# S5 tables' products and weighted adaLN sums on VectorE alone, with a four-operation S5 scan step on GpSimd, in a two-layer hybrid diffusion backbone

## The chip, the cores and the metric

One core of one Trainium2 chip runs the whole program. The metric is device microseconds for one execution. PE is TensorE (with PEld for its weight loads), DVE is VectorE, ACT is ScalarE, POOL is GpSimd, SP is the engine whose queue issues most of the DMAs.

## The reference

Two layers work on 512 tokens of 1024 channels: 256 of context and 256 of latents. Each layer takes a shift, a scale and a gate from the conditioning vector (one for the latents, another for the context), modulates an RMSNorm with them, projects it to all inputs of three mixers, merges the mixers by gates, and runs a SwiGLU FFN with the same kind of modulation:

```python
for l in range(DEPTH):                                   # DEPTH = 2
    mod = (silu_c @ w_ada[l] + b_ada[l])[:, None, :]     # 1024 -> 6 x 1024, latents
    mod_c = silu_cc @ w_ada[l] + b_ada[l]                # the same for the context
    ...
    u, rk, rv, nk, nv, rq, rg, nq, gates = split_cols(h @ w_in[l], IN_SPLIT)
    ...
    y_s5, y_s5_c = s5_mixer(u, cu, ...)    # both directions, 32 groups, 64 complex states each
    ...                                    # retention, neighbourhood attention, merge, FFN
```

The S5 mixer is a linear recurrence x[t] = a x[t-1] + B u[t] with complex a, forward and backward in time, followed by a read-out with C. All is fp32.

## The kernel before

**Weights.** Every weight is read once from HBM, in chunks of 512 KB (128 partitions x 1024 values) that SP's queue fetches into four raw buffers (L373). `w` turns a chunk into two fp32r tensors: the high part is a cast on ScalarE (L383), the low part a subtraction on VectorE (L384). `mm3` then issues three matmuls for each block of 128x128 weights: high by high (L389), high by low (L390), low by high (L391). So each chunk that is multiplied costs one ScalarE and one VectorE instruction over 128x1024 values, and TensorE waits for both.

**S5.** The recurrence is cut into chunks of eight tokens. Tables of products of powers of a with B (`s5_e`) and with C (`s5_g`, called by `s5_kwins` and `s5_out`) let TensorE do the work inside a chunk; `_prods` builds them, for four blocks of groups in each layer and each table. One call of `_prods` covers two directions, d = 0 and 1, with three instructions each: two products (L742, L743) and their sum or difference (L744), over 128x1024 values for `s5_e` and 128x1152 for `s5_g`. Direction 0 runs on VectorE and direction 1 on GpSimd. TensorE transposes the `s5_e` tables (L759); it multiplies the `s5_g` tables in `s5_kwin` (L1150). What is left between chunks is a scan of 64 steps (`s5_scan`), both directions at once, wholly on GpSimd: from the second step on, each takes three instructions over 128x64 values (L1094 to L1096) and two over 128x32 (L1097, L1098). After the last step the scan swaps halves of its result through memory called "swap": two DMAs (L1103, L1104) and two copies of 64x2112 values (L1105, L1106). It runs beside the neighbourhood attention's projections in each layer.

**adaLN of the second layer.** `ada_sum` runs beside the FFN of the first layer: 40 chunks of w_ada (five rounds of eight) are weighted by a column of the conditioning vector and summed, one sum for each of two vectors (s = 0 and 1). The first chunk of a round is a ScalarE multiplication (L559). For the other 35, s = 1 is one VectorE multiply-add (L561), while s = 0 is a ScalarE multiplication into a temporary (L565) and a GpSimd addition (L566). A few matmuls (L572) reduce the sums over the partitions.

**The order of the work.** The program is written as generators. `weave` interleaves a main generator with side generators at given rates (for the FFN of the first layer: `rest`, with `s5_e` and `s5_kwins` of the second layer, at 0.5, and the adaLN at 0.9). Buffers come from an allocator written for this kernel. A scheduler then sets the order on each engine's queue from its own estimate of the times. Each engine takes its queue strictly in order. `take(ada, ...)` in the second layer draws on the generator of `ada_sum`.

```python
weave(self.ffn(l, lambda: self.norm(l + 1, 0, [0, 1])), (rest(), 0.5), (chain(ada, self.adas), 0.9))
```

Of the kernel before, what the change touches and what calls it, by code (L numbers as in the profile page):

```python
# [13 lines left out]
ALU = mybir.AluOpType  # L14
# [51 lines left out]
def _consts():  # L66
# [27 lines left out]
def _layout(inp):  # L94
# [105 lines left out]
def mk(ap, off, dims):  # L200
    return bass.AP(ap.tensor, ap.offset + off, [list(ap.ap[0])] + [list(d) for d in dims])


def weave(main, *sides):

    acc = [0.0] * len(sides)
    live = [True] * len(sides)

    def step(i):
        try:  # L210
            next(sides[i][0])
        except StopIteration:
            live[i] = False

    for _ in main:
        for i, (_, each) in enumerate(sides):
            acc[i] += each
            while live[i] and acc[i] >= 1.0:
                acc[i] -= 1.0
                step(i)  # L220
    while any(live):
        for i in range(len(sides)):
            if live[i]:
                step(i)
# [6 lines left out]
def chain(*gens):  # L231
    for g in gens:
        yield from g


class Net:
# [10 lines left out]
    def run(self, stack):  # L247
        tc, nc = self.tc, self.nc
        NR = 8192 + 6 * 1024 + 8192
        NF = 30600  # L250
        sb = stack.enter_context(tc.tile_pool(name="sb", bufs=1))
        ps = stack.enter_context(tc.tile_pool(name="ps", bufs=1, space=PSUM))
        dr = stack.enter_context(tc.tile_pool(name="dr", bufs=1, space=DRAM))
        fa = sb.tile([P, NF], F32, name="fa")
        ra = sb.tile([P, NR], F32R, name="ra")
# [26 lines left out]
        def ld(name, n):  # L282
# [31 lines left out]
                                in1=cvec.rearrange("p (k s) -> p k s", s=2), op=ALU.mult)  # L314
# [234 lines left out]
    def ada_sum(self, l, rounds):  # L549

        nc, F = self.nc, self.F
        acc = [F.alloc(1024, "acc", top=True) for _ in range(2)]
        for r in rounds:
            for k in range(8):
                t = self.wraw(("w_ada", l, r, k))
                for s in range(2):
                    c = self.c32[:, k, s:s + 1]
                    if k == 0:
                        nc.scalar.mul(acc[s].ap, t, c)  # L559
                    elif s:  # L560
                        nc.vector.scalar_tensor_tensor(out=acc[s].ap, in0=t, scalar=c, in1=acc[s].ap,  # L561
                                                       op0=ALU.mult, op1=ALU.add)
                    else:
                        p = F.alloc(1024, "adap")
                        nc.scalar.mul(p.ap, t, c)  # L565
                        nc.gpsimd.tensor_tensor(out=acc[s].ap, in0=acc[s].ap, in1=p.ap, op=ALU.add)  # L566
                        p.free()
                yield
            pt = self.misc()
            for s in range(2):  # L570
                for q in range(4):
                    nc.tensor.matmul(pt[32 * q:32 * q + 32, 0:256], self.sel[:, s * 32:(s + 1) * 32],  # L572
                                     acc[s].v(256, q * 256), start=(s == 0), stop=(s == 1))
# [155 lines left out]

    def _prods(self, dst, A, B, c0, l, blk, nb, op):  # L730

        n0 = nb - 1
        P2 = self.tabs[l][0].ap
        for d in range(2):
            tmp = self.F.alloc(nb * 128, "prod")
            eng = (self.nc.vector, self.nc.gpsimd)[d]
            po = (n0 * 64 if d else 0) + blk * 16 + d
            pd = [[2, 8], [-64 if d else 64, nb], [0, 16]]
            wo, wd = c0 + d * 16, [[32, 8], [0, nb], [1, 16]]
            o = mk(dst, d * nb * 16, [[2 * nb * 16, 8], [16, nb], [1, 16]])  # L740
            t = tmp.ap.rearrange("p (g n h) -> p g n h", g=8, n=nb)
            eng.tensor_tensor(out=o, in0=mk(P2, po, pd), in1=mk(A, wo, wd), op=ALU.mult)  # L742
            eng.tensor_tensor(out=t, in0=mk(P2, 640 + po, pd), in1=mk(B, wo, wd), op=ALU.mult)  # L743
            eng.tensor_tensor(out=o, in0=o, in1=t, op=op)  # L744
            tmp.free()
# [147 lines left out]
    def layer(self, l):  # L893
        nc, F = self.nc, self.F
# [3 lines left out]
        na = [None, None]  # L898
        self.yna = self.yslot[0]
        if l == 0:  # L900
# [16 lines left out]
            ada = self.ada(0, (2, 3, 4, 5))  # L917
# [22 lines left out]
        else:  # L940
# [10 lines left out]
            for _ in self.m_u(l):  # L951
                pass
            weave(self.m_na(l, 0, na, kpre), (chain(*(self.s5_in(l, blk) for blk in range(4)), self.s5_scan(l)), 20))
            ada = self.adas
            weave(self.m_na(l, 1, na), (self.attn(l, 0, na), 2.5), (self.take(ada, 4), 0.5))
            self.yret = self.yslot[1]
            weave(self.m_ret(l), (self.attn(l, 1, na), 1.2), (self.ret_decay(l), 0.75), (self.take(ada, 4), 0.3))
            self.swap.free()
            self.m = F.alloc(8 * n, "m", top=True)
            weave(self.branch(l, 2, self.yna, 0), (self.retention(l), 2.5), (self.take(ada, 4), 0.25))  # L960
            tg = F.alloc(8 * n, "tg", top=True)
            ys5 = self.yslot[0][:, 1024:]
            weave(chain(self.branch(l, 1, self.yret, 1), self.gates(l, 0, tg)),
                  (chain(self.s5_out(l, self.yslot[0]), self.s5_glu(l, self.yslot[0], ys5)), 1), (self.take(ada, 3), 0.15))
            self.ug.free()
            self.X.free()
            self.x_alloc()
# [5 lines left out]
        ada = self.adas  # L973
        if last:
            ada = self.ada(1, (5,))
# [6 lines left out]
        else:  # L982
            e = []
# [83 lines left out]
    def s5_scan(self, l):  # L1067


        nc = self.nc  # L1070
        e = nc.gpsimd
        xb = self.X.ap
        self.swap = self.F.alloc(2112, "swap", top=True)
        A = [mk(self.PW, (ri * 10 + 8) * 64 + l * 32, [[0, 2], [1, 2], [2, 16]]) for ri in range(2)]
        T = [self.scan_tmp.v(64, 64 * i).rearrange("p (r d g) -> p r d g", r=2, d=2) for i in range(4)]

        def at(f, r, part=None):
            dims = [[1056 + (r - f) * 16, 2], [1, 16]]
            if part is None:
                return mk(xb, f * 16, [[2112, 2]] + dims)  # L1080
            return mk(xb, part * 2112 + f * 16, dims)

        for s in range(64):
            if s < 32:
                cf, cr = s + 1, 31 - s
                pf, pr = cf - 1, cr + 1
            else:
                cf, cr = s + 2, 96 - s
                pf, pr = cf - 1, cr + 1
            if s == 32:  # L1090
                e.tensor_copy(at(33, 65), at(32, 0))
            t1, t2 = T[(s % 2) * 2], T[(s % 2) * 2 + 1]
            if s:
                e.tensor_tensor(out=t1, in0=at(pf, pr), in1=A[0], op=ALU.mult)  # L1094
                e.tensor_tensor(out=t2, in0=at(pf, pr), in1=A[1], op=ALU.mult)
                e.tensor_tensor(out=at(cf, cr), in0=at(cf, cr), in1=t1, op=ALU.add)  # L1096
                e.tensor_tensor(out=at(cf, cr, 0), in0=at(cf, cr, 0), in1=t2[:, 1], op=ALU.subtract)  # L1097
                e.tensor_tensor(out=at(cf, cr, 1), in0=at(cf, cr, 1), in1=t2[:, 0], op=ALU.add)  # L1098
            yield
        self.dump(f"S{l}", self.X.ap)  # L1100

        tm = self.swap
        e.dma_start(tm.ap[0:64], xb[64:128, 0:2112])  # L1103
        e.dma_start(tm.ap[64:128], xb[0:64, 2112:4224])  # L1104
        e.tensor_copy(xb[64:128, 0:2112], tm.ap[64:128])  # L1105
        e.tensor_copy(xb[0:64, 2112:4224], tm.ap[0:64])  # L1106
        yield
# [723 lines left out]
```

## Time and profile before

| | |
|---|---|
| median of 3 runs | 1609.64 us (1609.52 to 1610.44) |
| the profiled execution's own time | 1614.29 us |
| its span, first to last instruction | 1612.5 us |
| mean granted TensorE clock | 0.972 of full speed |
| busy: PE / DVE / ACT / POOL | 1506.2 / 1024.7 / 663.5 / 473.4 us |
| read from and written to HBM | 226 MB and 16 MB, 150 GB/s over the span |

The profile is one execution. "Busy" is the time in which an engine ran instructions; an instruction that waits for a resource inside its run counts as busy. A wait of an engine is put down to the instruction that released it. The granted clock is a share of TensorE's full speed, 2.4 GHz.

### The profile page before, as it was taken

How to read it: one execution, taken by the hardware profiler on the slowest of the kernel's cores; microseconds unless marked ns; L12 is line 12 of the kernel's file. 1: busy time of each engine (PE TensorE's matmuls, PEld its weight loads, DVE VectorE, ACT ScalarE, POOL GpSimd, SP SyncE). 2: the span in 40 equal slices, each digit the busy share in tenths (PEclk: the TensorE clock that was granted, in tenths of full speed). 3: DMA queues.
4: the chain of work that ended last, by engine and by line, in shares of the span. 5: the costliest groups of instructions: out<-in, count | busy, mean ns of one | idle time of the engine just before them, and what ended most of it. 6: DMA issues, size and time to landing. Idle time of an engine off the chain costs nothing.

```text
span 1612.5 us, 25768 instructions
## 1 busy us (share of the span) xinstructions
PE 1506.2 (93%) x10066; PEld 1272.9 (79%) x10066; DVE 1024.7 (64%) x1716; ACT 663.5 (41%) x1166; POOL 473.4 (29%) x750
## 2 busy tenths in 40 slices
PE   7968999899999999989997989999996999999997
PEld 5756677678888887777885768898785999899997
DVE  6794435657456686689588895551662765765566
ACT  4525444224422334343432343445643445454443
POOL 0083985530000020157155660005994000000000
PEclk9989999999999999999998999999997999999999
DMA  9412345564332423544444653332322686655552
GB/s 371 140 37 102 119 151 174 169 196 160 124 105 79 155 81 121 167 169 157 146 167 158 214 165 121 111 129 83 105 88 74 201 278 234 222 183 184 183 180 96
DMA packets 78587, 245.94 MB, mean 153 GB/s; under 512 B 9088, under 2 KB 22912, under 8 KB 76672
## 3 DMA queue, kind: packets, MB, share of 16 engines
q1 hardware_dynamic: 76864, 237.92, 44.0%
q0 software_dynamic: 1600, 6.36, 1.3%
q8 instruction: 79, 1.29, 0.3%
q14 instruction: 44, 0.36, 0.1%
HBM read 225.96 MB, written 16.12 MB: 150 GB/s over the span
## 4 chain that ended last, share of the span: by engine, by line
PE 67%; DVE 9%; POOL 7%; issue 7%; DMA 6%; ACT 3%; SPq 1%; DVEq 0%; POOLq 0%; ACTq 0%
PE psall L389 17%; PE psall L391 17%; PE psall L390 17%; DMA fa<-in_wst_dram 3%; DVE ra L384 3%; PE psall L867 2%; PE psall L869 2%; PE psall L868 2%; DVE fa L561 2%; POOL fa L744 1%; POOL fa L743 1%; PE psall L517 1%; PE psall L1054 1%; PE psall L1215 1%; POOL fa L1097 1%
## 5 line engine op out<-in xcount | busy, mean ns | idle before, releaser
L389 PE MATMUL psall<-ra 128*128 128x256 f32 (+1 forms) x2122 | 713.7, 341 | 18.4 <-ACT ra L383 15.4
L391 PE MATMUL psall<-ra 128*128 128x256 f32 (+1 forms) x2122 | 710.5, 338 | 13.3 <-DVE ra L384 13.3
L390 PE MATMUL psall<-ra 128*128 128x256 f32 (+1 forms) x2122 | 712.0, 337 | 0.0
L384 DVE TENSOR_TENSOR ra<-fa,ra 128x1024 fp32r<-128x1024 f32 (+1 forms) x284 | 384.1, 1355 | 296.9 <-ACT ra L383 294.8
L383 ACT CAST ra<-fa 128x1024 fp32r<-128x1024 f32 (+1 forms) x284 | 293.5, 1036 | 472.7 <-PE psall L390 249.6
L389 PEld LDWEIGHTS psall<-ra 128*128 128x128 f32 x2122 | 403.9, 192 | 74.4 <-ACT ra L383 18.2
L391 PEld LDWEIGHTS psall<-ra 128*128 128x128 f32 x2122 | 405.7, 192 | 58.4 <-DVE ra L384 17.2
L390 PEld LDWEIGHTS psall<-ra 128*128 128x128 f32 x2122 | 407.1, 192 | 41.9 <-issue 3.3
L566 POOL TENSOR_TENSOR fa<-fa 128x1024 f32<-128x1024 f32 x35 | 101.1, 2889 | 161.3 <-DMA fa<-in_wst_dram 70.7
L742 POOL TENSOR_TENSOR fa<-fa 128x1024 f32<-128x1024 f32 (+1 forms) x16 | 49.3, 3086 | 286.6 <-DVE fa L699 244.2
L561 DVE SCALAR_TENSOR_TENSOR fa<-fa 128x1024 f32<-128x1024 f32 x35 | 77.6, 2218 | 8.5 <-ACT fa L559 5.7
L867 PE MATMUL psall<-ra 128*128 128x512 f32 x192 | 76.2, 409 | 5.5 <-ACT ra L828 4.9
L868 PE MATMUL psall<-ra 128*128 128x512 f32 x192 | 75.9, 399 | 0.0
L565 ACT ACTIVATE fa<-fa 128x1024 f32<-128x1024 f32 x35 | 40.2, 1151 | 83.8 <-DMA fa<-in_wst_dram 37.1
L869 PE MATMUL psall<-ra 128*128 128x512 f32 x192 | 72.5, 400 | 0.2 <-DVE ra L829 0.2
L1698 DVE SCALAR_TENSOR_TENSOR fa<-psall,fa 128x256 f32<-128x256 f32 x96 | 43.2, 477 | 45.6 <-PE psall L391 45.4
L1094 POOL TENSOR_TENSOR fa<-fa 128x64 f32<-128x64 f32 x126 | 44.4, 353 | 81.4 <-ACT fa L1062 71.8
L743 POOL TENSOR_TENSOR fa<-fa 128x1024 f32<-128x1024 f32 (+1 forms) x16 | 46.3, 2893 | 45.6 <-DVE fa L744 20.1
L867 PEld LDWEIGHTS psall<-ra 128*128 128x128 f32 x192 | 43.6, 229 | 12.7 <-ACT ra L828 5.9
L744 POOL TENSOR_TENSOR fa<-fa 128x1024 f32<-128x1024 f32 (+1 forms) x16 | 52.3, 3269 | 0.6
L868 PEld LDWEIGHTS psall<-ra 128*128 128x128 f32 x192 | 44.1, 230 | 5.5 <-DVE ra L384 0.4
L1096 POOL TENSOR_TENSOR fa<-fa 128x64 f32<-128x64 f32 x126 | 47.1, 374 | 0.0
(252 smaller groups left out, 1623.3 us busy)
## 6 DMA issues: line engine op xcount, KB each, us to landing
fa<-in_wst_dram SPq DMA_DIRECT2D x364, 512.0 KB, 3.7
fa<-in_wst_dram SPq DMA_DIRECT2D x16, 384.0 KB, 3.0
gsp<-fa SPq DMA_DIRECT2D x4, 1152.0 KB
fa<-gsp SPq DMA_DIRECT2D x4, 1152.0 KB, 9.2
xsp<-fa SPq DMA_DIRECT2D x2, 2048.0 KB
tgs<-fa POOLq DMA_DIRECT2D x16, 256.0 KB, 3.7
fa<-kws SPq DMA_DIRECT2D x32, 128.0 KB
fa<-tgs SPq DMA_DIRECT2D x16, 256.0 KB, 3.0
```

Source lines behind the costliest of these rows:

```text
L383: nc.scalar.copy(hi[:, :n], t[:, :n])
L384: nc.vector.tensor_tensor(out=lo[:, :n], in0=t[:, :n], in1=hi[:, :n].bitcast(F32), op=ALU.subtract)
L389: mm(out, wh, xh, start=start, stop=False)
L390: mm(out, wh, xl, start=False, stop=False)
L391: mm(out, wl, xh, start=False, stop=stop)
L561: nc.vector.scalar_tensor_tensor(out=acc[s].ap, in0=t, scalar=c, in1=acc[s].ap, op0=ALU.mult, op1=ALU.add)
L566: nc.gpsimd.tensor_tensor(out=acc[s].ap, in0=acc[s].ap, in1=p.ap, op=ALU.add)
L743: eng.tensor_tensor(out=t, in0=mk(P2, 640 + po, pd), in1=mk(B, wo, wd), op=ALU.mult)
L744: eng.tensor_tensor(out=o, in0=o, in1=t, op=op)
L867: mm(o, xh, hi[:, ws], start=(kk == 0), stop=False)
L868: mm(o, xh, lo[:, ws], start=False, stop=False)
L869: mm(o, xl, hi[:, ws], start=False, stop=(kk == 7))
```

## The change

Three places change. `_prods` runs both directions on VectorE. `ada_sum` does both sums with the VectorE multiply-add; the ScalarE multiplication, its temporary and the GpSimd addition go. `s5_scan` first writes a table of 128 values, [re, re | im, -im] of the power for both directions, with four ScalarE multiplications (L1074 in the changed file); a step is then four GpSimd instructions over 128x64 values: two products and two additions, the second of which reads its operand with real and imaginary parts exchanged. The scan's scratch grows from 256 to 384 values, the arena from 30600 to 30680. The `take(ada, ...)` sides of the second layer go. In the changed file a line behind L565 has a number lower by 4 or 5 (L742 to L744 are L737 to L739).

```diff
@@ ada_sum
                     if k == 0:
                         nc.scalar.mul(acc[s].ap, t, c)
-                    elif s:
+                    else:
                         nc.vector.scalar_tensor_tensor(out=acc[s].ap, in0=t, scalar=c, in1=acc[s].ap,
                                                        op0=ALU.mult, op1=ALU.add)
-                    else:
-                        p = F.alloc(1024, "adap")
-                        nc.scalar.mul(p.ap, t, c)
-                        nc.gpsimd.tensor_tensor(out=acc[s].ap, in0=acc[s].ap, in1=p.ap, op=ALU.add)
-                        p.free()
@@ _prods
-            eng = (self.nc.vector, self.nc.gpsimd)[d]
+            eng = self.nc.vector
@@ layer 1 of run
-            weave(self.m_na(l, 1, na), (self.attn(l, 0, na), 2.5), (self.take(ada, 4), 0.5))
+            weave(self.m_na(l, 1, na), (self.attn(l, 0, na), 2.5))
...
@@ s5_scan
+        tab = self.scan_tmp.v(128, 256)
+        pw = lambda ri: self.PW[:, (ri * 10 + 8) * 64 + l * 32:(ri * 10 + 8) * 64 + l * 32 + 32].rearrange(
+            "p (g d) -> p d g", d=2)
+        for i in range(4):
+            nc.scalar.mul(tab[:, i * 32:(i + 1) * 32].rearrange("p (d g) -> p d g", d=2), pw(i // 2),
+                          -1.0 if i == 3 else 1.0)
...
-                e.tensor_tensor(out=t1, in0=at(pf, pr), in1=A[0], op=ALU.mult)
-                e.tensor_tensor(out=t2, in0=at(pf, pr), in1=A[1], op=ALU.mult)
-                e.tensor_tensor(out=at(cf, cr), in0=at(cf, cr), in1=t1, op=ALU.add)
-                e.tensor_tensor(out=at(cf, cr, 0), in0=at(cf, cr, 0), in1=t2[:, 1], op=ALU.subtract)
-                e.tensor_tensor(out=at(cf, cr, 1), in0=at(cf, cr, 1), in1=t2[:, 0], op=ALU.add)
+                for i in range(2):
+                    e.tensor_tensor(out=t[:, i], in0=at(pf, pr),
+                                    in1=tab[:, i * 64:(i + 1) * 64].rearrange("p (r d g) -> p r d g", r=2, d=2),
+                                    op=ALU.mult)
+                e.tensor_tensor(out=at(cf, cr), in0=at(cf, cr), in1=t[:, 0], op=ALU.add)
+                e.tensor_tensor(out=at(cf, cr), in0=at(cf, cr),
+                                in1=mk(T[s % 2], 96, [[-32, 2], [16, 2], [1, 16]]), op=ALU.add)
```

The scheduler moves instructions too. On VectorE, at the tables of `s5_e` in the first layer, before (L699 belongs to the table of B; "ra" is the arena of the fp32r tensors, "fa" the fp32 arena):

```order
L742 TENSOR_TENSOR fa<-fa 128x8x128
L699 TENSOR_TENSOR fa<-fa 128x1024
L743 TENSOR_TENSOR fa<-fa 128x1024
L742 TENSOR_TENSOR fa<-fa 128x8x128
L743 TENSOR_TENSOR fa<-fa 128x1024
L744 TENSOR_TENSOR fa<-fa 128x8x128 x2
```

and now:

```order
L737 TENSOR_TENSOR fa<-fa 128x8x128 x2
L694 TENSOR_TENSOR fa<-fa 128x1024
L738 TENSOR_TENSOR fa<-fa 128x1024 x2
L737 TENSOR_TENSOR fa<-fa 128x8x128
L738 TENSOR_TENSOR fa<-fa 128x1024
L737 TENSOR_TENSOR fa<-fa 128x8x128
L738 TENSOR_TENSOR fa<-fa 128x1024
L739 TENSOR_TENSOR fa<-fa 128x8x128 x3
```

Before, the first sum (L744) of direction 0 is the sixth instruction here, and direction 1 is in GpSimd's queue. Now the products of several directions and blocks come first; the sums of the first block, both directions, are the tenth and eleventh.

On ScalarE, in the second layer where the scan ends, before (L1559 copies retention queries into the memory that "swap" left, L1483 and L1398 belong to the projections and the attention, L1551 copies the retention's context state):

```order
L1327 ACTIVATE fa<-psall,fa 128x256 [waits DVE_49,PE_49]
L1328 ACTIVATE fa<-fa 128x256 [waits Activation_49]
L1559 COPY fa<-fa 64x256 [waits DMASW3_49,Pool_49]
L1559 COPY fa<-fa 64x256 x3
L383 CAST ra<-fa 128x1024 [waits DMAHW0_49,PE_49]
L1483 ACTIVATE fa<-psall 128x256 [waits PE_49]
L1551 COPY fa<-psall 128x512 [waits PE_49]
```

and now:

```order
L1323 ACTIVATE fa<-psall,fa 128x256 [waits DVE_49,PE_49,Activation_49]
L1324 ACTIVATE fa<-fa 128x256
L1555 COPY fa<-fa 64x256 x2
L383 CAST ra<-fa 128x1024 [waits DMAHW0_49,PE_49]
L1479 ACTIVATE fa<-psall 128x256 [waits PE_49]
L1547 COPY fa<-psall 128x512 [waits DMASW2_49,DMASW3_49,PE_49,Pool_49]
```

The wait for GpSimd's swap (Pool and its DMAs) moved from the first query copy to the copy of the context state, behind one more cast of a weight chunk.

Also on ScalarE, in the first layer where the scan ends, the changed program has the second layer's table of powers, whose memory is the first layer's scratch:

```order
L1323 ACTIVATE fa<-psall,fa 128x256 [waits DVE_49,PE_49]
L1324 ACTIVATE fa<-fa 128x256
L1074 ACTIVATE fa<-fa 128x32 [waits Pool_49]
L1074 ACTIVATE fa<-fa 128x32
L1074 ACTIVATE fa<-fa 128x32 [waits Pool_49]
L1074 ACTIVATE fa<-fa 128x32
L405 CAST ra<-psall 128x512 [waits PE_49]
L383 CAST ra<-fa 128x1024 [waits DMAHW4_49,PE_49,Activation_49]
```

These four have no counterpart before; their first and third wait for the last products of the first layer's scan, and the cast of a weight chunk stands behind them.

On TensorE, at the C part's tables in the first layer, three weight matmuls stand between the last adaLN reduction of `_ada` (L517) and the first multiplication with the table (L1150) before, 39 now.

## Rows read from the trace of the kernel before

**Rows 1.** The page: busy time of each engine, share of the span.

```profile
PE 1506.2 (93%) x10066; PEld 1272.9 (79%) x10066; DVE 1024.7 (64%) x1716; ACT 663.5 (41%) x1166; POOL 473.4 (29%) x750
```

**Rows 2.** Waits of PE: releaser, us in total, times, longest us.

```profile
PE psall L389 <- ACT ra L383: 15.4, 4, 13.4
PE psall L391 <- DVE ra L384: 13.3, 9, 4.0
PE psall L759 <- DVE fa L744: 11.6, 1, 11.6
PE psall L1150 <- DVE fa L744: 7.5, 2, 5.0
PE psall L1150 <- POOL fa L744: 6.6, 2, 5.5
...
PE psall L572 <- POOL fa L566: 4.0, 2, 2.3
```

**Rows 3.** Timeline of DVE, first tables: start us, us, instruction.

```profile
80.02 1.21 DVE L742 TENSOR_TENSOR fa<-fa 128x1024 f32<-128x1024 f32 x1
...
86.51 3.04 DVE L743 TENSOR_TENSOR fa<-fa 128x1024 f32<-128x1024 f32 x1
```

**Rows 4.** Timeline of POOL in the same stretch; in brackets the idle time before.

```profile
75.25 2.03 POOL L742 TENSOR_TENSOR fa<-fa 128x1024 f32<-128x1024 f32 x1 [18.36 <-DVE fa L699]
...
85.47 3.00 POOL L742 TENSOR_TENSOR fa<-fa 128x1024 f32<-128x1024 f32 x1
```

**Rows 5.** Timeline of PE: transposes of the first tables.

```profile
94.77 2.61 PE L759 MATMUL psall<-fa 128*128 128x128 f32 x11 [1.72 <-POOL fa L744]
```

**Rows 6.** Windows: start:end, us; busy of PE, PEld, DVE, ACT, POOL; PEclk, DMA, GB/s.

```profile
293.00:300.00 7.00, 7.00 (x24) 5.38 (x25) 7.00 (x3) 0.18 (x1) 6.13 (x3) 0.74 0.39 157
570.00:1000.00 430.00, 398.03 (x2036) 320.82 (x2035) 329.22 (x328) 167.08 (x219) 175.24 (x59) 0.97 0.46 153
690.00:970.00 280.00, 252.21 (x1222) 198.84 (x1221) 229.34 (x177) 108.26 (x131) 156.24 (x53) 0.96 0.50 170
...
1222.00:1236.00 14.00, 0.72 (x7) 0.48 (x5) 0.00 (x0) 2.60 (x6) 6.71 (x11) 0.61 0.40 97
1236.00:1246.00 10.00, 9.43 (x58) 8.44 (x59) 3.21 (x4) 3.65 (x10) 0.00 (x0) 0.70 0.14 54
```

**Rows 7.** Timeline of POOL: layer 1's scan, a step and the final copy.

```profile
1209.36 0.32 POOL L1094 TENSOR_TENSOR fa<-fa 128x64 f32<-128x64 f32 x1
...
1209.92 0.32 POOL L1096 TENSOR_TENSOR fa<-fa 128x64 f32<-128x64 f32 x1
1210.32 0.25 POOL L1097 TENSOR_TENSOR fa<-fa 128x32 f32<-128x32 f32 x1
...
1210.86 0.32 POOL L1094 TENSOR_TENSOR fa<-fa 128x64 f32<-128x64 f32 x1
...
1233.37 1.94 POOL L1106 COPY fa<-fa 64x2112 f32<-64x2112 f32 x1
```

**Rows 8.** Timeline of ACT: the query copies of layer 1's retention.

```profile
1233.34 1.64 ACT L1559 COPY fa<-fa 64x256 f32<-64x256 f32 x4 [15.98 <-POOL fa L1105]
```

**Rows 9.** Groups by shape on DVE and POOL, 690 to 970: count, busy, mean ns.

```profile
L384 DVE TENSOR_TENSOR ra<-fa,ra 128x1024 fp32r<-128x1024 f32 x42 | 80.1, 1908 | 23.4 <-ACT ra L383 23.3
L561 DVE SCALAR_TENSOR_TENSOR fa<-fa 128x1024 f32<-128x1024 f32 x31 | 68.5, 2209 | 4.1 <-ACT fa L559 2.5 <-DMA fa<-in_wst_dram 1.4
...
L566 POOL TENSOR_TENSOR fa<-fa 128x1024 f32<-128x1024 f32 x33 | 96.2, 2916 | 80.4 <-ACT fa L559 47.4 <-ACT fa L565 32.1
```

**Rows 10.** Source line L561: duration ns minimum/median/maximum, first and last start.

```profile
L561 DVE SCALAR_TENSOR_TENSOR fa<-fa x35: 1269/2222/3537, 663.5 to 966.2; 128x1024 f32<-128x1024 f32 x35
```

**Rows 11.** Timelines of POOL and ACT: layer 0's scan, first and last instruction; next cast.

```profile
143.68 0.32 POOL L1094 TENSOR_TENSOR fa<-fa 128x64 f32<-128x64 f32 x1 [25.80 <-ACT fa L1062]
...
255.22 0.25 POOL L1098 TENSOR_TENSOR fa<-fa 128x32 f32<-128x32 f32 x1
...
249.49 0.59 ACT L405 CAST ra<-psall 128x512 fp32r<-128x512 f32 x1 [2.53 <-PE psall L1425]
```

More of the change, by code (lines that the diff above doesn't have):

```diff
@@ L249, in run @@
         NR = 8192 + 6 * 1024 + 8192
-        NF = 30600
+        NF = 30680
         sb = stack.enter_context(tc.tile_pool(name="sb", bufs=1))
@@ L318, in run @@
         self.lg = F.alloc(16, "lg", top=True).ap
-        self.scan_tmp = F.alloc(256, "scan", top=True)
+        self.scan_tmp = F.alloc(384, "scan", top=True)
         self.x_alloc()
@@ L954, in layer @@
             ada = self.adas
-            weave(self.m_na(l, 1, na), (self.attn(l, 0, na), 2.5), (self.take(ada, 4), 0.5))
+            weave(self.m_na(l, 1, na), (self.attn(l, 0, na), 2.5))
             self.yret = self.yslot[1]
-            weave(self.m_ret(l), (self.attn(l, 1, na), 1.2), (self.ret_decay(l), 0.75), (self.take(ada, 4), 0.3))
+            weave(self.m_ret(l), (self.attn(l, 1, na), 1.2), (self.ret_decay(l), 0.75))
             self.swap.free()
             self.m = F.alloc(8 * n, "m", top=True)
-            weave(self.branch(l, 2, self.yna, 0), (self.retention(l), 2.5), (self.take(ada, 4), 0.25))
+            weave(self.branch(l, 2, self.yna, 0), (self.retention(l), 2.5))
             tg = F.alloc(8 * n, "tg", top=True)
@@ L963, in layer @@
             weave(chain(self.branch(l, 1, self.yret, 1), self.gates(l, 0, tg)),
-                  (chain(self.s5_out(l, self.yslot[0]), self.s5_glu(l, self.yslot[0], ys5)), 1), (self.take(ada, 3), 0.15))
+                  (chain(self.s5_out(l, self.yslot[0]), self.s5_glu(l, self.yslot[0], ys5)), 1))
             self.ug.free()
@@ L1073, in s5_scan @@
         self.swap = self.F.alloc(2112, "swap", top=True)
[L1074 to L1081, printed above, removed]
-        for s in range(64):
[L1084 to L1089, printed above, removed]
+        tab = self.scan_tmp.v(128, 256)
@@ new lines, in s5_scan, with at @@
+        pw = lambda ri: self.PW[:, (ri * 10 + 8) * 64 + l * 32:(ri * 10 + 8) * 64 + l * 32 + 32].rearrange(
[3 more added lines that the diff above has]
+                          -1.0 if i == 3 else 1.0)
+        T = [self.scan_tmp.v(128, 128 * i) for i in range(2)]
+        def at(f, r):
+            return mk(xb, f * 16, [[2112, 2], [1056 + (r - f) * 16, 2], [1, 16]])
+        for s in range(64):
+            cf, cr = (s + 1, 31 - s) if s < 32 else (s + 2, 96 - s)
+            pf, pr = cf - 1, cr + 1
@@ L1090, in s5_scan @@
             if s == 32:
                 e.tensor_copy(at(33, 65), at(32, 0))
-            t1, t2 = T[(s % 2) * 2], T[(s % 2) * 2 + 1]
+            t = T[s % 2].rearrange("p (a r d g) -> p a r d g", a=2, r=2, d=2)
             if s:
-                e.tensor_tensor(out=t1, in0=at(pf, pr), in1=A[0], op=ALU.mult)
-                e.tensor_tensor(out=t2, in0=at(pf, pr), in1=A[1], op=ALU.mult)
-                e.tensor_tensor(out=at(cf, cr), in0=at(cf, cr), in1=t1, op=ALU.add)
-                e.tensor_tensor(out=at(cf, cr, 0), in0=at(cf, cr, 0), in1=t2[:, 1], op=ALU.subtract)
-                e.tensor_tensor(out=at(cf, cr, 1), in0=at(cf, cr, 1), in1=t2[:, 0], op=ALU.add)
+                for i in range(2):
[5 more added lines that the diff above has]
+                                in1=mk(T[s % 2], 96, [[-32, 2], [16, 2], [1, 16]]), op=ALU.add)
```

## The prediction

> **What bounds the kernel now.** I read the page first: TensorE is busy for 1506 of 1612.5 us, VectorE for 1025, GpSimd for 473 [rows 1]. So 106 us are TensorE's idle time, and only that, and the slow clock behind it, can be won. The view of TensorE's waits says for whom it stood still [rows 2]. Six of its rows, 58 us together, name instructions that the change touches or that stand in a queue with them: the tables' sums (L744), the low parts of weights (L384), the adaLN additions (L566), and the cast L383 in its longest wait, 13.4 us. That wait has another cause than the row names: ScalarE stood idle for 15.98 us just then, until GpSimd's swap copy L1105 released the query copies that stand ahead of the cast [rows 8].
>
> Then I looked at why the tables are slow. VectorE's product L742 at 80 us, with GpSimd idle, takes 1.21 us; a product of the same size at 86.5 us, with GpSimd in a product of its own, takes 3.04 [rows 3]. GpSimd's takes 2.03 alone and 3.00 then [rows 4]. Side by side, each lasts about as long as both alone, 1.21 + 2.03 = 3.24. The two engines take turns: what GpSimd does on these shapes VectorE pays for. The weighted sums show the same: L561 lasts 1.27 us at best and 2.22 in the median [rows 10], and L384 has a mean of 1.91 in the stretch where GpSimd does 33 additions of 2.92 us [rows 9].
>
> [...]
>
> **The change part by part.** All sums are against the profiled execution's 1614.3 us, which is 4.65 above the median of the runs.
>
> *Tables of the first layer's B part* (75 to 119 us). Twelve instructions leave GpSimd, VectorE gets them: 24 x 1.21 = 29 us in one queue, where twelve pairs at 3.0 made 36. But the new order puts the sums of the first block tenth and eleventh, behind products of other blocks. From 80.0 us eleven instructions at 1.21 end at 93.3, against TensorE's start at 94.77 [rows 5]; the 11.6 us wait [rows 2] stays nearly whole. I take the 1.5 us and the 1.7 us for which TensorE then waited for GpSimd: **3 us**, between 0 (products first, so later blocks are no earlier) and 8 (the stage's whole shortening, 36 - 29).
>
> *Tables of the first layer's C part* (278 to 300 us). TensorE waited 5.0 us for VectorE's sum [rows 2], then ran at a granted clock of 0.74 for 7 us [rows 6], which cost 7.0 x 0.26 = 1.8. In the changed order 39 weight matmuls stand between the adaLN sums and the first multiplication with the table, where three did. They fill the wait, if their chunk's low part comes in time: two chunks' worth of work stands there and the tables are 1.36 us each now (1.21 x 1152/1024) instead of 3.4. **7 us**, between 2 (a low part queued behind the tables) and 9.
>
> *The scan.* An undisturbed step starts every 1.50 us: 0.28 for each independent product, 0.40 to an instruction that needs the one before, 0.54 for the last two and the start of the next [rows 7]. The new step has two products and two dependent additions: 0.28 + 0.28 + 0.40 + 0.40 = 1.36, if the second addition over 64 values costs like the first. That is 63 x 0.14 = 8.8 us; the first layer's scan took 111.8 us where 63 x 1.50 = 94.5 [rows 11], so with its blocked share 8.8 x 1.18 = 10.4. In the first layer nobody waits for the scan's end in the views read: 0. In the second the swap's last copy ends at 1233.37 + 1.94 = 1235.3 [rows 7] and would end at 1224.9. TensorE ran out of work 13.4 us before 1236.1, at 1222.7 [rows 2]; it is busy for 0.72 of the 14 us from 1222 [rows 6]. The wait for the swap moves, by the new order, behind one more cast, which gives TensorE one more chunk. So of 13.4 us some 1 to 2 are left, and of the 2.8 us lost after it (9.43 busy at a clock of 0.70 [rows 6]) most returns: **14 us**, between 3 (the step is no shorter; only the extra chunk helps) and 17.
>
> *Four ScalarE multiplications for the table of powers.* In the second layer's case they wait, in ScalarE's queue, for the first layer's last products, with casts queued behind. By 1.36 x 63 x 1.18 = 101 the scan would end at 245; the conversion that stands behind them ran at 249.5 [rows 11]. At 0.2 to 0.5 us each they are covered by ScalarE's idle 2.5 us there: 0; were the scan not shorter, they would hold the casts until 255, some 6 us.
>
> *The adaLN sums and the second layer's tables* (570 to 1000 us). TensorE is busy 398 of 430 us here [rows 6], 32 idle, and the clock of 0.97 costs another 10. The change takes 35 ScalarE and 35 GpSimd instructions and half the tables away and gives VectorE 35 multiply-adds and 21 of the tables' instructions. VectorE's load from 690 to 970, at undisturbed durations: 42 L384 x 1.21 = 51; 64 multiply-adds (31 and 33) x 1.27 = 81; 42 tables' instructions (seven of eight calls, 18 x 1.21 + 24 x 1.36) = 54; the rest some 40 of the 229 now busy: 226, against 229 [rows 6]. So VectorE does GpSimd's work in the time for which it was blocked. It stays at 80% or more, and some of TensorE's waits for L384 [rows 2] stay; those for GpSimd (6.6 and 4.0) go, and with them the chains by which ScalarE waited for an addition to free a temporary. I take half of the idle 32 and 4 of clock: **20 us**, between 5 (less than GpSimd's waits alone) and 38.
>
> *The scratch and the dropped sides.* The generator is used up within the first layer (L561 ends at 966 us [rows 10]): 0.
>
> Sum: 3 + 7 + 14 + 20 = 44. 1614.3 - 44 = 1570.3, and 4.65 less for the median: **1566 us**.
>
> **The rivals.**
>
> *VectorE becomes the bound in the FFN.* Two multiply-adds in a row (2.5 us) now stand ahead of each L384, in order. For it: 226 us of 280, and nine waits for L384 already. Against it: one blocked multiply-add cost 2.2. Then the last term is 0: 1570.3 + 20 - 4.65 = 1586.
>
> *All of it returns.* The idle time and clock of all four stages: 8 + 9 + 17 + 38 = 72, 1538. Against it: VectorE's load is no smaller than before.
>
> *Slower.* The 2.2 us of L561 and the 1.9 of L384 are their own price, from their shapes or weight traffic, and GpSimd's part in them is nothing. Then VectorE needs 106 x 2.09 = 222 us for both kinds plus 54 and 40: 316, for a stretch of 280, and with the 23 us that it waits for casts [rows 9] some 340: 60 lost there, 24 won elsewhere: 1614.3 + 36 - 4.65 = 1646. It turns slower than before from a mean of 1.8 us for those 106 instructions (106 x 1.8 + 94 + 23 = 308, 28 over the stretch). Against it: 1.27 us at best, for the same shape.
>
> *The change does not do what it says.* If the scan's step is bound by its instructions' dependence and stays at 1.50, and the powers' table holds ScalarE for 6 us, while the FFN gives nothing: 3 + 7 + 3 - 6 = 7, hardly more than a measurement can tell (about 0.2%, 3 us): 1603.
>
> **How the numbers follow.** The forecast has 0.70, VectorE as the bound 0.17, all returned 0.06, slower 0.04, little done 0.03. The range of 8 in 10 is 1540 to 1590: it takes the second case in and the forecast's own bounds, though not all at once, and leaves out the last two, the third's far end and the tails. Faster by over 0.2%: 0.70 + 0.17 + 0.06 + 0.01 of little done, 0.94; the same 0.02; slower 0.04.
>
> **What would show it.** VectorE's tables at 1.2 to 1.4 us and L561 near 1.3 with no 3 us among them; GpSimd busy for some 190 us, nearly all scan; a step every 1.36 us; the swap's last copy some 10 us earlier against TensorE's work, and no wait of 13 us there; TensorE idle some 65 us, with its waits for GpSimd gone and its wait for the first table still near 10. It is wrong if L561 stays above 2 us, if TensorE's waits for L384 grow past 30 us, or if ScalarE stands at the powers' table.

## The result, and the profile after

The changed kernel takes 1574.68 us (median of 4 runs, 1571.81 to 1577.81) where the kernel before takes 1610.04: a ratio of 0.978 with a 95% interval of 0.9761 to 0.980. It is faster, as forecast, inside the range and 8.7 us above the number given. The profiled execution took 1571.81 us with a span of 1570.0, 42.5 us less than the profiled execution before; the medians differ by 35.4. The sums below go by the two profiles.

The page of the changed kernel, its busy times (against [rows 1]):

```profile
PE 1494.5 (95%) x10066; PEld 1270.5 (81%) x10066; DVE 988.2 (63%) x1799; ACT 632.2 (40%) x1139; POOL 204.2 (13%) x541
```

GpSimd gave up 269 us, and VectorE, which took the work over, is busy for 36.5 us less than before. TensorE's idle time fell from 106 to 75.5 us. The waits of TensorE (against [rows 2]):

```profile
PE psall L754 <- DVE fa L739: 10.5, 2, 9.8
PE psall L1146 <- DVE fa L739: 7.0, 2, 5.5
...
PE psall L1544 <- DVE fa L1536: 6.1, 1, 6.1
...
PE psall L389 <- DVE fa L1152: 3.7, 2, 3.4
...
PE psall L389 <- ACT ra L383: 3.3, 5, 1.1
...
PE psall L391 <- DVE ra L384: 1.8, 1, 1.8
```

The waits for GpSimd are gone, those for the weights' halves (L383, L384) fell from 28.7 to 5.1 us, the one for the first table is nearly what it was, and two rows are new: L1544 behind L1536, and L389 behind L1152. Source lines L561 and L384 (durations in ns: minimum/median/maximum; against [rows 9, 10]):

```profile
L561 DVE SCALAR_TENSOR_TENSOR fa<-fa x70: 1277/1283/1297, 659.6 to 926.4; 128x1024 f32<-128x1024 f32 x70
```

```profile
L384 DVE TENSOR_TENSOR ra<-fa,ra x284: 948/1226/1358, 19.3 to 1554.4; 128x1024 fp32r<-128x1024 f32 x134, 128x768 fp32r<-128x768 f32 x8
```

All 70 multiply-adds lie within 20 ns of each other, where 35 had lain between 1.27 and 3.54 us; no L384 lasts above 1.36 us, where some had lasted 3.4. Windows of the changed kernel (columns as in [rows 6]):

```profile
330.00:350.00 20.00, 9.54 (x54) 6.38 (x53) 14.04 (x16) 2.00 (x5) 0.00 (x0) 0.59 0.41 134
570.00:1000.00 430.00, 425.77 (x2229) 348.83 (x2228) 324.37 (x421) 140.51 (x204) 0.00 (x0) 0.99 0.49 162
690.00:970.00 280.00, 278.16 (x1389) 223.31 (x1388) 218.52 (x246) 86.18 (x114) 0.00 (x0) 0.99 0.54 178
1184.00:1200.00 16.00, 10.08 (x72) 9.64 (x74) 6.32 (x10) 5.12 (x11) 3.88 (x2) 0.79 0.21 66
```

In the FFN of the first layer TensorE is now busy for 425.8 of 430 us (398.0 before). But there is a new hole at 330 to 350 us, in which it works for 9.5 of 20 us at a clock of 0.59 of full speed (between its levels of 1.2 and 2.4 GHz), and one at 1184 to 1200.

To see where a kernel gains, I use the casts L383 as milestones, since every kernel here multiplies the same chunks of weights: the start of the 65th (after the first layer's mixers), of the 137th (after its FFN), and the end of the span. The first two in the timelines of ScalarE, before and then after:

```profile
542.84 1.05 ACT L383 CAST ra<-fa 128x1024 fp32r<-128x1024 f32 x1 [3.89 <-issue]
...
1009.08 0.84 ACT L383 CAST ra<-fa 128x768 fp32r<-128x768 f32 x1 [3.30 <-PE psall L390]
```

```profile
541.33 1.05 ACT L383 CAST ra<-fa 128x1024 fp32r<-128x1024 f32 x1 [3.89 <-issue]
...
970.65 0.84 ACT L383 CAST ra<-fa 128x768 fp32r<-128x768 f32 x1 [3.30 <-PE psall L390]
```

So of the 42.5 us the first layer's mixers give 1.5, its FFN 36.9 and all the rest 4.1. That is not how the sum was made up (10, 20 and 14). All kernels in one table: median, ratio to the kernel before with its interval (against the runs of that kernel which were taken with it, medians of 1610.0 to 1612.0), and the change of each stretch in the profiled execution, in us. A stretch is read from one execution, and the runs of one kernel differ by 4 to 12 us, so a few us between two rows of a stretch say little.

| kernel | median us | ratio (95%) | to cast 65 | to cast 137 | to the end |
|---|---|---|---|---|---|
| changed kernel | 1574.7 | 0.978 (0.9761 to 0.9800) | -1.5 | -36.9 | -4.1 |
| e1_tables | 1580.7 | 0.9816 (0.9798 to 0.9834) | -15.1 | -21.1 | +0.7 |
| e2_adaln | 1593.1 | 0.9888 (0.9869 to 0.9907) | -3.3 | -30.0 | +8.3 |
| e3_scan | 1626.3 | 1.0099 (1.0082 to 1.0115) | +6.0 | -4.1 | +9.2 |
| e9_padonly | 1636.5 | 1.0144 (1.0116 to 1.0172) | +17.5 | -1.7 | +8.8 |
| e7_small | 1572.3 | 0.9746 (0.9717 to 0.9774) | -9.8 | -36.5 | +7.7 |
| e13_beforelate | 1604.0 | 0.9957 (0.9941 to 0.9973) | +1.2 | -1.8 | -9.4 |
| e4_swaplate | 1562.9 | 0.9725 (0.9688 to 0.9761) | -1.7 | -37.1 | -13.8 |
| e7_smalllate | 1557.5 | 0.9637 (0.9597 to 0.9678) | -10.1 | -39.4 | -7.2 |
| e8_oldscan | 1575.1 | 0.9762 (0.9735 to 0.9789) | -11.2 | -40.3 | +11.1 |
| e10_oldscanlate | 1554.6 | 0.9650 (0.9625 to 0.9676) | -11.3 | -38.3 | -9.8 |
| e11_tablesback | 1574.9 | 0.9772 (0.9757 to 0.9787) | -4.1 | -29.5 | -5.7 |
| e12_adaback | 1576.7 | 0.9781 (0.9759 to 0.9803) | -7.2 | -19.7 | -8.7 |

### The profile page after: what moved, and what is told of

It is laid out like the page before. It is cut to its first block, busy times and chain, and to the rows that moved or that the text cites. A ratio compares the mean times of both kernels' runs of the same rounds, so it can differ in the third digit from the quotient of the medians.

```text
span 1570.0 us, 25507 instructions
## 1 busy us (share of the span) xinstructions
PE 1494.5 (95%) x10066; PEld 1270.5 (81%) x10066; DVE 988.2 (63%) x1799; ACT 632.2 (40%) x1139; POOL 204.2 (13%) x541
## 4 chain that ended last, share of the span: by engine, by line
PE 88%; DMA 4%; DVE 4%; ACT 2%; issue 1%; SPq 0%; POOL 0%; POOLq 0%; DVEq 0%; ACTq 0%
PE psall L389 23%; PE psall L391 22%; PE psall L390 22%; PE psall L862 3%; PE psall L864 3%; PE psall L863 3%; DMA fa<-in_wst_dram 2%; PE psall L1049 1%; PE psall L1363 1%; PE psall L1398 1%; PE psall L1370 1%; PE psall L517 1%; PE psall L1211 1%; PE psall L754 1%; PE psall L1570 1%
## 5 line engine op out<-in xcount | busy, mean ns | idle before, releaser
L389 PE MATMUL psall<-ra 128*128 128x256 f32 (+1 forms) x2122 | 713.7, 341 | 10.5 <-DVE fa L1152 3.7
L384 DVE TENSOR_TENSOR ra<-fa,ra 128x1024 fp32r<-128x1024 f32 (+1 forms) x284 | 343.5, 1212 | 297.8 <-ACT ra L383 282.8
L383 ACT CAST ra<-fa 128x1024 fp32r<-128x1024 f32 (+1 forms) x284 | 293.7, 1037 | 564.4 <-PE psall L390 327.7
L389 PEld LDWEIGHTS psall<-ra 128*128 128x128 f32 x2122 | 402.9, 191 | 68.4 <-issue 11.7
L391 PEld LDWEIGHTS psall<-ra 128*128 128x128 f32 x2122 | 405.0, 191 | 45.4 <-issue 3.1
L390 PEld LDWEIGHTS psall<-ra 128*128 128x128 f32 x2122 | 406.0, 191 | 39.5 <-issue 1.1
L1089 POOL TENSOR_TENSOR fa<-fa 128x64 f32<-128x64 f32 x252 | 90.5, 380 | 139.0 <-ACT fa L1057 129.4
L561 DVE SCALAR_TENSOR_TENSOR fa<-fa 128x1024 f32<-128x1024 f32 x70 | 87.6, 1283 | 8.5 <-DMA fa<-in_wst_dram 8.2
L862 PEld LDWEIGHTS psall<-ra 128*128 128x128 f32 x192 | 43.5, 229 | 13.2 <-ACT ra L823 5.8
L1092 POOL TENSOR_TENSOR fa<-fa 128x64 f32<-128x64 f32 x126 | 50.5, 400 | 0.0
L1093 POOL TENSOR_TENSOR fa<-fa 128x64 f32<-128x64 f32 x126 | 48.0, 381 | 9.8
L863 PEld LDWEIGHTS psall<-ra 128*128 128x128 f32 x192 | 43.9, 230 | 4.9
L864 PEld LDWEIGHTS psall<-ra 128*128 128x128 f32 x192 | 42.0, 229 | 5.8 <-issue 0.4
L738 DVE TENSOR_TENSOR fa<-fa 128x1024 f32<-128x1024 f32 (+1 forms) x32 | 40.4, 1288 | 7.4 <-DMA fa<-in_s5c_dram 7.3
L405 ACT CAST ra<-fa 128x512 fp32r<-128x512 f32 (+1 forms) x52 | 26.5, 510 | 41.6 <-DVE fa L1760 29.1
```

The costliest lines, as they stand in the source:

```text
L383: nc.scalar.copy(hi[:, :n], t[:, :n])
L384: nc.vector.tensor_tensor(out=lo[:, :n], in0=t[:, :n], in1=hi[:, :n].bitcast(F32), op=ALU.subtract)
L389: mm(out, wh, xh, start=start, stop=False)
L390: mm(out, wh, xl, start=False, stop=False)
L391: mm(out, wl, xh, start=False, stop=stop)
L862: mm(o, xh, hi[:, ws], start=(kk == 0), stop=False)
```

## The experiments

**One part at a time.** e1_tables is the kernel before with one line changed:

```diff
-            eng = (self.nc.vector, self.nc.gpsimd)[d]
+            eng = self.nc.vector
```

> The kernel before with only the tables' products moved to VectorE. Theory (the engines take turns, so what leaves GpSimd costs VectorE little): tables at 1.22 and 1.36 us wherever no GpSimd addition runs beside them, the first layer's stages some 10 us shorter; in the first layer's FFN the 35 GpSimd additions stay and still block VectorE (L561 above 2 us), which now has 21 to 24 instructions more, so little or nothing is won there: 1600 us (1590 to 1612). Rival (the turns matter nowhere but in the tables): the FFN gains its waits for L744 too, 1585 us.

Measured: 1580.7 us, 0.9816. The first layer gains the 15 us, more than I gave it, but the FFN gains 21 where I expected at most a few. L561 there:

```profile
L561 DVE SCALAR_TENSOR_TENSOR fa<-fa x35: 1272/1285/3534, 645.0 to 930.9; 128x1024 f32<-128x1024 f32 x35
```

23 of the 35 stay below 1.3 us now, where 17 did before, though GpSimd's additions are all still there. The measured time lies below the expected range. My expectation counted what the additions cost VectorE and left out what the tables' pairs had cost it: VectorE takes some 24 instructions more, but its own 24, at up to 3.4 us beside their partners, last 1.35 now. The rival's 1585 is nearer.

e2_adaln is the kernel before with the sum of s = 0 on VectorE:

```diff
-                    elif s:
+                    else:
                         nc.vector.scalar_tensor_tensor(...)
-                    else:
-                        ...
```

> The kernel before with only the weighted adaLN sums moved to VectorE. Theory: L561 falls from 2.2 to 1.3 us except beside a GpSimd table product, L384 in the FFN from 1.9 to some 1.3, and the FFN of the first layer is 25 us shorter (of the 37 that it became shorter in the changed kernel): 1585 us (1575 to 1595). Rival (VectorE is the bound there and only swaps waiting for work): 1605 us or more, with VectorE's load in the stretch as before and TensorE's idle time in it near 30 us.

Measured: 1593.1 us, 0.9888, inside the expected range. The FFN gains 30 us, and 8 are lost again behind cast 137. Most of these stand between the casts 181 and 193, in the second layer: 46.0 us from one to the other, where the kernel before took 40.1. ScalarE waits there for a chunk of weights, and TensorE 4.1 us for ScalarE:

```profile
1269.51 1.04 ACT L383 CAST ra<-fa 128x1024 fp32r<-128x1024 f32 x1 [10.05 <-DMA fa<-in_wst_dram]
```

The rival falls: at 70 multiply-adds VectorE does not become the bound, and TensorE is idle for 10.7 us in the FFN (540 to 976 us), not for 30.

e3_scan is the kernel before with the new scan, its scratch and its arena:

> The kernel before with only the four-operation scan step and its table of powers. Theory: the step starts every 1.36 us, the second layer's scan ends about 10 us earlier, TensorE's 13.4 us wait there falls to some 4 to 6 and nothing else moves: 1601 us (1597 to 1606). Rival (the step is a minor matter, TensorE's wait is put down to it by the order of ScalarE's queue only): 1609 to 1611 us with a shorter scan.

Measured: 1626.3 us, 1.0099. Slower, and both theories miss it. The step does start every 1.36 us (timeline of GpSimd in e3_scan, second layer; 1.35 in the changed kernel):

```profile
1215.52 0.60 POOL L1094 TENSOR_TENSOR fa<-fa 128x64 f32<-128x64 f32 x2
1216.08 0.33 POOL L1097 TENSOR_TENSOR fa<-fa 128x64 f32<-128x64 f32 x1
1216.48 0.32 POOL L1098 TENSOR_TENSOR fa<-fa 128x64 f32<-128x64 f32 x1
1216.88 0.59 POOL L1094 TENSOR_TENSOR fa<-fa 128x64 f32<-128x64 f32 x2
```

Yet TensorE's wait at the swap is as long as before. ScalarE and then TensorE in e3_scan:

```profile
1227.43 1.64 ACT L1560 COPY fa<-fa 64x256 f32<-64x256 f32 x4 [16.82 <-POOL fa L1106]
```

```profile
1231.29 0.69 PE L1403 MATMUL psall<-fa 128*64 128x128 f32 x2 [14.32 <-ACT fa L1399]
```

The query copies stand one cast earlier in ScalarE's queue than in the kernel before (behind 168 casts L383, not 169). The scheduler, which plans with a shorter scan, put them there, and the wait came along. And the first layer lost 6 us before any of that, which asked for the next experiment.

**The scratch.** e9_padonly changes two numbers of the kernel before and no instruction:

```diff
-        NF = 30600
+        NF = 30680
-        self.scan_tmp = F.alloc(256, "scan", top=True)
+        self.scan_tmp = F.alloc(384, "scan", top=True)
```

> The kernel before with nothing changed but the sizes: scan scratch 384 instead of 256, arena 30680 instead of 30600, the scan and all else as before. Theory (the scan's scratch takes 48 values from the rest of the arena, the tiles of the first layer's C tables fall on other memory, and their loads wait for it and stand behind weight loads in SP's queue): TensorE is stalled between 310 and 370 us as in the changed kernel and in e3_scan, and the kernel is slower than before by 10 to 18 us: 1624 us (1619 to 1630). Rival (the stall comes from the scan's earlier end or from VectorE's tables): as before, 1608 to 1613 us.

Measured: 1636.5 us, 1.0144: 24 us slower for 48 values fewer in the rest of the arena, the largest loss of the whole series. Waits of TensorE in e9_padonly:

```profile
PE psall L389 <- ACT ra L383: 22.3, 7, 15.1
PE psall L391 <- DVE ra L384: 11.9, 7, 3.9
PE psall L759 <- DVE fa L744: 11.6, 1, 11.6
PE psall L1150 <- DVE fa L744: 10.8, 5, 5.1
```

Against [rows 2] the wait for the C tables' sums by VectorE grew from two places to five. The longest of the five, 5.1 us, stands at 869 us, in the FFN. In the first layer's C part it is the whole stretch that got worse: windows from 310 to 370 us of the kernel before and of e9_padonly (columns as in [rows 6]).

```profile
310.00:370.00 60.00, 57.75 (x559) 42.86 (x557) 31.47 (x41) 16.70 (x31) 20.47 (x11) 1.00 0.62 197
```

```profile
310.00:370.00 60.00, 49.91 (x505) 37.24 (x500) 35.31 (x36) 15.03 (x25) 23.45 (x11) 0.94 0.64 216
```

Not all of the 17.5 us up to cast 65 is this: 5.4 of them were lost before 216 us, where the granted clock was lower (0.86 against 1.00 from 50 to 75 us, 0.85 against 0.96 from 160 to 200). The reason for the rest stands in SP's queue. The loads of C (L670 to L672) for the third block, in the kernel before and in e9_padonly:

```profile
301.95 0.38 SPq L670 DMA_DIRECT2D fa<-in_s5c_dram  x1
302.38 0.47 SPq L671 DMA_DIRECT2D fa<-in_s5c_dram  x1
302.91 0.59 SPq L672 DMA_DIRECT2D fa<-in_s5c_dram  x1
```

```profile
331.50 0.80 SPq L670 DMA_DIRECT2D fa<-in_s5c_dram  x1
332.39 1.07 SPq L373 DMA_DIRECT2D fa<-in_wst_dram  x2
333.86 0.52 SPq L671 DMA_DIRECT2D fa<-in_s5c_dram  x1
334.43 0.58 SPq L672 DMA_DIRECT2D fa<-in_s5c_dram  x1
```

With less room the tiles fall on memory that is still in use, the loads have to wait for it, and they are queued behind weight loads that wait themselves (L671 stood for 4.5 us until TensorE's L1215 released it). In the changed kernel the same happens, and it shows how far one late load reaches (SP, then VectorE, then TensorE):

```profile
318.19 8.83 SPq L373 DMA_DIRECT2D fa<-in_wst_dram  x3
327.11 0.52 SPq L666 DMA_DIRECT2D fa<-in_s5c_dram  x1
```

```profile
318.41 2.63 DVE L737 TENSOR_TENSOR fa<-fa 128x1152 f32<-128x1152 f32 x2
...
332.40 1.36 DVE L738 TENSOR_TENSOR fa<-fa 128x1152 f32<-128x1152 f32 x1 [5.14 <-DMA fa<-in_s5c_dram]
...
335.54 1.35 DVE L739 TENSOR_TENSOR fa<-fa 128x1152 f32<-128x1152 f32 x1
```

```profile
336.95 0.63 PE L1146 MATMUL psall<-fa 128*32 128x128 f32 x2 [5.45 <-DVE fa L739]
...
344.55 0.79 PE L389 MATMUL psall<-ra 128*128 128x512 f32 x1 [3.45 <-DVE fa L1152]
```

The products of the third block were done by 321 us. Their sum, L739 at 335.5, stands in VectorE's queue behind a product of the fourth block (L738), which waits for its C, which waits in SP's queue behind three weight loads. With direction 1 on VectorE too, all of it is in one queue.

e3_scan, with the same sizes as e9_padonly and the shorter scan, is 10 us faster than it. All of that lies before cast 137 (the stretch behind it is equal, 9.2 against 8.8), and 4.4 us of it are there at 216 us already, ahead of the C part; what the rest is was not tested.

e7_small is the changed kernel with one temporary for the products of all steps, so that scratch and arena have their old sizes:

```diff
-        NF = 30680
+        NF = 30600
-        self.scan_tmp = F.alloc(384, "scan", top=True)
+        self.scan_tmp = F.alloc(256, "scan", top=True)
-        tab = self.scan_tmp.v(128, 256)
+        tab = self.scan_tmp.v(128, 128)
-        T = [self.scan_tmp.v(128, 128 * i) for i in range(2)]
+        T = [self.scan_tmp.v(128)] * 2
```

> The changed kernel with a scan scratch of 256 values (the two products' temporaries of all steps share one tile) and the arena of 30600, so that the rest of the arena is as before. Theory: the C tables' loads come early again, the stall of 310 to 370 us goes, and 15 to 20 of the changed kernel's 1574.7 us are won: 1556 us (1552 to 1563). Rival (the shared temporary makes the scan's step longer, or the stall stays): 1570 to 1580 us.

Measured: 1572.3 us, only 2.4 less than the changed kernel, within the two kernels' spread and in the rival's range. Half of the theory holds: to cast 65 it gains 8 us on the changed kernel, and TensorE is busy for the whole of 330 to 350. But the end loses 12. ScalarE, and TensorE's waits, in e7_small:

```profile
1178.66 1.64 ACT L1555 COPY fa<-fa 64x256 f32<-64x256 f32 x4 [13.17 <-POOL fa L1101]
```

```profile
PE psall L1398 <- ACT fa L1394: 11.6, 3, 9.6
```

It is the swap again: the order has changed once more and the query copies are back in front of the swap.

**The swap.** The retention's tiles reuse the memory of "swap", which the program frees just before the retention. e13_beforelate is the kernel before, e4_swaplate the changed kernel, with one line moved:

```diff
-            self.swap.free()
             self.m = F.alloc(8 * n, "m", top=True)
             weave(self.branch(l, 2, self.yna, 0), (self.retention(l), 2.5), ...)
+            self.swap.free()
```

> The kernel before with the swap's memory freed after the second layer's retention and nothing else. Theory (the 13.4 us wait at 1236 us is one for memory, not for the scan's result): it goes without a shorter scan, with the slow clock behind it: 1596 us (1592 to 1600). Rival (the scan's result itself is waited for soon after, or the wait moves on): 1605 to 1612 us.

Measured: 1604.0 us, 0.9957, between the two expectations; 7 us are won by the medians, 10 by the profiles (expected 15). Waits of TensorE in e13_beforelate:

```profile
PE psall L391 <- DVE ra L384: 14.7, 10, 4.0
PE psall L759 <- DVE fa L744: 11.6, 1, 11.6
...
PE psall L389 <- ACT ra L383: 5.4, 6, 2.3
```

The 13.4 us wait of [rows 2] is gone with the old scan in place. So it was a wait for memory. ScalarE's query copies now start 22 us before GpSimd's last swap copy ends (ScalarE, then GpSimd):

```profile
1217.90 1.64 ACT L1559 COPY fa<-fa 64x256 f32<-64x256 f32 x4
```

```profile
1237.58 2.83 POOL L1106 COPY fa<-fa 64x2112 f32<-64x2112 f32 x1
```

By the casts the kernel is 16 us ahead just behind it and 10 in the end; 4.7 of the other 6 go between the casts 181 and 193 again (44.8 us against 40.1).

> The changed kernel with the swap's memory freed after the second layer's retention instead of before it, so that no retention tile is put there. Theory (what is left of the scan's wait is a wait for memory: TensorE's 6.1 us behind L1536, which waits for the swap's last copy): that wait goes, TensorE's L1544 starts 6 us earlier, and with the slow clock behind it 6 to 9 us are won on the changed kernel's 1574.7: 1567 us (1563 to 1571). Rival (the scan's result is needed then anyway, or the next wait takes its place): 1572 to 1577 us.

Measured: 1562.9 us, 0.9725, 12 us less than the changed kernel, a little more than expected, though its runs spread from 1561.8 to 1573.2. The wait for L1536 is gone. In the changed kernel it read so (VectorE, then TensorE):

```profile
1188.58 1.29 DVE L1536 TENSOR_TENSOR fa<-psall,fa 128x512 f32<-128x512 f32 x2 [8.65 <-POOL fa L1102]
```

```profile
1189.92 3.78 PE L1544 MATMUL psall<-fa 128*128 128x128 f32 x16 [6.13 <-DVE fa L1536]
```

L1536 scales the retention's keys and needs nothing of the scan; its tile lay on the swap's memory.

> e7_small and the swap's memory freed after the second layer's retention (e4_swaplate). Theory: the two gains add, 15 to 20 and 12 of 1574.7: 1545 us (1540 to 1552). Rival (one hides the other): 1553 to 1560 us.

Measured (e7_small with that line moved): 1557.5 us, 0.9637, 17 less than the changed kernel, where the sum was 30: the rival's range. The swap's wait is gone. Of the small scratch's gain a part is kept: against e4_swaplate the kernel is 10.8 us ahead at cast 137 and 4.2 at the end.

**The parts undone, with both faults mended.** e8_oldscan is the changed kernel with scan, scratch and arena of before; e10_oldscanlate is that with the swap freed late.

> The changed kernel with the scan, its scratch and the arena of before: only the tables and the adaLN sums are moved. Theory: the first layer's tables give the 15 us of e1_tables, its FFN the 37 of the changed kernel, and only the swap's wait in the second layer is longer than in e7_small, by 2 to 8 us: 1560 us (1554 to 1566), so the four-operation step itself is worth little and its scratch costs more than it brings. Rival (the step is worth its 10 us): e7_small's time and 10 to 14 us more.

Measured: 1575.1 us, as the changed kernel and e7_small; the expectation was 15 too low, in the main for the reason that e7_small's was: the swap's wait (here TensorE's longest wait for the cast L383, 10.5 us). The rest is lost behind it: from cast 181 to 193 the kernel takes 50.8 us, e10_oldscanlate 44.6.

> The tables and adaLN sums on VectorE, the swap's memory freed late, the scan, its scratch and the arena as before. Theory (once nobody waits for the swap, the scan's length is covered): e7_smalllate's time within its spread, 1556 us (1551 to 1562). Rival (the four-operation step is worth its 10 us by itself): 1564 to 1570 us.

Measured: 1554.6 us, 0.965 against e7_smalllate's 0.9637, intervals overlapping nearly whole. The four-operation step, 10 us shorter over a scan, is worth nothing that can be seen once nothing waits for the swap's memory. e10_oldscanlate, with the old scan, is as good as any kernel here, 20 us ahead of the changed one (the ratios' intervals do not touch).

The other two undo a part of e7_smalllate: e11_tablesback puts direction 1 of `_prods` back on GpSimd, e12_adaback the sum of s = 0 back on ScalarE and GpSimd.

> e7_smalllate with direction 1 of the tables' products back on GpSimd. Theory (turns): the first layer's tables lose the 15 us that e1_tables won, the FFN of the first layer some 7 (37 to 30), together 22: 1579 us (1573 to 1585). Rival (the moved work fills VectorE, so half of it elsewhere is no worse): 1555 to 1562 us.

Measured: 1574.9 us, in the expected range; 17 are lost: 6 in the first layer (expected 15) and 10 in the FFN (expected 7).

> e7_smalllate with the first adaLN sum back on ScalarE and GpSimd. Theory: only the first layer's FFN changes, it loses the difference between 37 and the 21 that e1_tables won there: 1573 us (1567 to 1579); L561 in two groups, near 1.28 us and near 3. Rival: 1555 to 1562 us.

Measured: 1576.7 us, 19 lost, in the FFN nearly all, as expected. L561 in e12_adaback:

```profile
L561 DVE SCALAR_TENSOR_TENSOR fa<-fa x35: 1271/1284/3527, 653.6 to 940.0; 128x1024 f32<-128x1024 f32 x35
```

The longest is 3.5 us again. Each part alone gives 20 or 30 of the FFN's 37 to 39 us. The timelines show what they have in common. Take each TENSOR_TENSOR and SCALAR_TENSOR_TENSOR of VectorE between the casts 65 and 137 that lasts over 0.1 us longer than the shortest of its shape, and add up the excess: 94 us in the kernel before, 54 in e1_tables, 57 in e12_adaback, 39 in e2_adaln and e11_tablesback, 0 in the changed kernel. The FFN's gains follow in that order: 0, 21, 20, 30 and 30, 37.

## Why the prediction was right, and where it was not

The reason given for the whole was right: the two engines take turns, so what leaves GpSimd costs VectorE little. VectorE's load from 690 to 970 us was worked out as 226 us and measured 218.5; L561 at 1.27 became 1.283; the tables last 1.22 and 1.35 us, and e1_tables, which moves the tables alone, gains 15 us up to cast 65. The Trainium skill's "SBUF — State Buffer", section "SBUF: two separate sides", has a rule for this: a VectorE instruction with two SBUF inputs and a GpSimd instruction that reads SBUF lock each other out for a whole instruction. The traces agree: 3.04 us for a product beside one of GpSimd, 1.21 without.

*Tables of the B part*: 3 us forecast, 2.7 measured, in part by luck. TensorE's first transpose moved from 92.57 to 89.86 us, behind the tenth instruction, and the other fifteen follow behind the eleventh, as the order said; the wait is still 9.8. But the sum set its 93.3 us against 94.77, where the fifteen had started, and against the first transpose's 92.57 it gave no gain. What made up for it: the products start every 1.14 us and not every 1.21, and the first starts at 78.24 and not 80.02, mainly since the L384 ahead of the tables lasts 1.22 us where it had lasted 2.35 beside a GpSimd product.

*Tables of the C part*: 7 forecast. The wait of 5.0 us did go, and TensorE's first L1211 stands 11 us earlier (302.9 against 314.2). But at cast 65 only 1.5 us of the B and C parts together are left. The step that failed is "The scratch and the dropped sides", which I put at 0. I looked at whether the sides were empty, and not at what 48 values less in the arena do to loads. The scratch alone costs 8 us there in the changed kernel (e7_small), and in the kernel before 12 of e9_padonly's 17.5.

*The scan*: 14 forecast, 4 measured. Its price was right: a step of 1.36 us, 101.8 us for the first layer's scan where 101 was forecast, no loss at the four multiplications (they waited 3.0 us on ScalarE, TensorE did not). What failed is the step from the scan's end to TensorE: "of 13.4 us some 1 to 2 are left". I followed the moved wait in ScalarE's queue and not in VectorE's, where L1536 now had it, and took a wait for the swap's memory as one for the scan. It is removed without a shorter scan (e13_beforelate), and the shorter scan without its removal brings nothing that can be seen (e7_small against e8_oldscan; in e3_scan the wait stays at 14.3 us).

*The adaLN sums and tables in the FFN*: 20 forecast, 36.9 measured, near my upper bound of 38. I halved the idle time because VectorE would stay at 80% load. It is at 78% (218.5 of 280), and TensorE waits for it 1.8 us in the whole FFN. Between the casts 65 and 137 TensorE's idle time fell from 32.0 to 4.2 us, where I took 16 off, and its busy time by 8.3 us, with the granted clock at 0.99 instead of 0.97, where I took 4. The rival "VectorE becomes the bound" rested on the same thought and is refuted. TensorE had waited there 15.4 us for VectorE (12.9 for low parts, 2.5 for a table) and 11.0 for GpSimd itself. VectorE's load is nearly what it was (229 and 218.5 us), so the waits for it came from single instructions of 2 to 3.5 us, not from the load.

So that the total held this well is luck: a term that was 17 too small and two that were 18 too large in sum cancelled.

## What to carry to other kernels

Where GpSimd and VectorE both read their operands from SBUF, on shapes like these, price an instruction on GpSimd as time taken from VectorE, and judge VectorE by its longest instruction ahead of a waiting TensorE as much as by its load. When a change touches the size of a buffer, look at where loads stand in their queue before and after: two numbers cost 24 us here with no instruction changed. And before making a producer faster, ask whether its consumer waits for the result or only for the memory; the second is mended by freeing it later.

## What was not expected of the hardware

The turns go the other way too, and for small instructions. In the changed kernel a scan addition, 0.32 us otherwise, lasts 1.19 us while VectorE is in an L384 (VectorE, then GpSimd):

```profile
1171.35 1.31 DVE L384 TENSOR_TENSOR ra<-fa,ra 128x1024 fp32r<-128x1024 f32 x1 [0.92 <-ACT ra L383]
```

```profile
1171.65 1.19 POOL L1093 TENSOR_TENSOR fa<-fa 128x64 f32<-128x64 f32 x1
```

It ends 0.18 us after VectorE's instruction, so it had waited for nearly all of it. And without GpSimd beside them, 70 VectorE instructions of one shape spread by no more than 20 ns.

Still open: why weight chunks and other loads come later between the casts 181 and 193 in e2_adaln, e9_padonly, e8_oldscan and e13_beforelate, where 5 to 11 us are lost; and the first table's wait of 9.8 us, for which the order of products and sums was not tried.
